# Gate and up projections as seven products of a 2x2 block product in a float32 encoder layer on one core

## The chip, the cores and the metric

The kernel runs on one core of one Trainium2 chip. The metric is the time of one execution on the device in microseconds (us). Three runs of the kernel before gave 1198.27, 1194.62 and 1189.96 us, a median of 1194.62 us. Inside the core five engines work side by side, each on its own queue in order: PE (TensorE, the products), DVE (VectorE), ACT (ScalarE), POOL (GpSimd) and SP, which here only issues transfers.

## The reference

One inference step of an encoder layer: a prompt of 512 tokens and 8 streams of 16 tokens, 640 tokens in all, width 1024. Two attention branches are merged by gates and projected; then comes the feed-forward part that the change is about:

```python
x = x + gate1 * ((gates[:, :, 0] * y_a + gates[:, :, 1] * y_b) @ w_out)
h = modulate(rmsnorm(x, g_norm_ffn), shift2, scale2)
return x + gate2 * ((jax.nn.silu(h @ w_gate) * (h @ w_up)) @ w_down)
```

`w_gate` and `w_up` are 1024 x 2816, `w_down` is 2816 x 1024. All is float32. The hidden width 2816 is 22 blocks of 128.

## The kernel before

Each float32 operand is split in two parts of PE's format: ACT rounds it to the high part (line 86), DVE or POOL subtracts that from the raw value, which gives the low part (line 87). A float32 product is then three matmuls: high by high, low by high, high by low (lines 93 to 95, `mm3`).

The feed-forward part runs over the 22 blocks of the hidden width. For a block `ff_weights` loads 512 KB of `w_gate` and 512 KB of `w_up` (8 slices of 128 x 128 each) into a ring of three raw buffers and splits each 128 x 1024 tile at once. `ff_block` takes 320 of the 640 tokens (tokens 0 to 319, then 320 to 639): 8 slices of the gate product into one PSUM bank, 8 of the up product into another, three matmuls each, then silu on ACT (line 1245), the product on DVE (line 1248) and the split into `aT`, `aTl`. That is 96 matmuls of 128 x 320 a block. After blocks 8, 16 and 22 the down projection adds its 512-column products to the residual `x1` (lines 1279 and 1280).

Ahead of it stands the output projection: for each of five tiles of 128 tokens 24 matmuls, then the new residual, its statistics (`h2_stats`: sum of squares, `rsqrt`, the scaled copy `xn`), and 8 transposes with the modulation and the split (`h2_cols`). `h2_cols(t - 1)` is called after `h2_stats(t)`. The first two blocks' first token half needs tiles 0 to 2 only. And ahead of that stands the merge of the two branches (`w_o_a`, `w_o_b`), whose first weights go into the raw ring `wstA`, which lives through the whole kernel.

The queues are laid out by a list scheduler from the program's text, its priorities and an estimate of each instruction; each engine then runs its list in order and waits on semaphores. So a row that waits holds back all rows behind it on its engine.

Of the kernel before, what the change touches and what calls it, by code (L numbers as in the profile page):

```python
# [8 lines left out]
F32 = mybir.dt.float32  # L9
# [39 lines left out]
def layer_kernel(  # L49
# [42 lines left out]
    def mm3(out, lh, ll, rh, rl, start, stop):  # L92
        T.matmul(out, lh, rh, start=start, stop=False)  # L93
        T.matmul(out, lh, rl, start=False, stop=False)  # L94
        T.matmul(out, ll, rh, start=False, stop=stop)  # L95
# [70 lines left out]
    wa = ctx.enter_context(pool("wstA", side="right"))  # L166

    def load_raw(src, shape, rows=P, given=P):
        n = shape[0] * shape[1]
        raw = wa.tile([P, 1024], F32, tag="w_raw", bufs=3, name=nm("wraw"))[:rows, :n]  # L170
        rv = raw.rearrange("p (k n) -> p k n", k=shape[0])
        if given < rows:
            G.memset(raw, 0.0)
        nc.sync.dma_start(rv[:given], src)
        return raw, rv

    def load_kv_up(c0):
        raw = wa.tile([P, 1024], F32, tag="w_raw", bufs=3, name=nm("wraw"))
# [897 lines left out]
    wb_cm = pool("wstB2", side="right")  # L1076
    wb = wb_cm.__enter__()
    AB = (wa, wb)
    gp_cm = pool("gatebc", side="right")
    gp = gp_cm.__enter__()  # L1080
# [6 lines left out]
    def ada_rows(c0):  # L1087
        raw = wa.tile([P, 1024], F32, tag="w_raw", bufs=3, name=nm("wraw"))
# [4 lines left out]
    def gate_rows(c0, scale):  # L1093

        raw = ada_rows(c0)
        hi = wa.tile([P, 1024], F32R, tag="w_hi", bufs=3, name=nm("whi"))[0:AR, :]
        lo = wa.tile([P, 1024], F32R, tag="w_lo", bufs=3, name=nm("wlo"))[0:AR, :]
        split(hi, lo, raw)
        out = []
        for v in range(2):  # L1100
            g_ = gp.tile([P, DM], F32, tag=f"gate{v}", name=nm("gate"))
            for c in range(2):
                cc = slice(c * 512, (c + 1) * 512)
                ps = mm_tile()
                T.matmul(ps, selr[:, v * P:(v + 1) * P], hi[:, cc], start=True, stop=False)  # L1105
                T.matmul(ps, selr[:, v * P:(v + 1) * P], lo[:, cc], start=False, stop=True)  # L1106
# [4 lines left out]
    with pool("mwork") as mw:  # L1111
# [10 lines left out]
        for bg in range(4):  # L1122
            wo = [granule(AB[br], wo_v[br][:, :, bg * 256:(bg + 1) * 256], [4, 256]) for br in range(2)]
            for bl in range(2):
# [35 lines left out]
    h2T = h2p.tile([P, KD, NT], F32R, tag="h2T", name="h2T")  # L1160
    h2Tl = h2p.tile([P, KD, NT], F32R, tag="h2Tl", name="h2Tl")
# [4 lines left out]
    sq = ow.tile([P, 2, TT], F32, tag="sq", name="sq")  # L1166
    xns = {}

    def h2_stats(t):
# [4 lines left out]
        xn = ow.tile([P, DM], F32, tag="xn", bufs=2, name=nm("xn"))  # L1174
# [3 lines left out]
    def h2_cols(t):  # L1178
        tsl = slice(t * P, (t + 1) * P)
        for b in range(2):  # L1180
# [19 lines left out]
            split(h2T[:, kb_, tsl], h2Tl[:, kb_, tsl], hf_.rearrange("p (k n) -> p k n", k=4))  # L1200
# [4 lines left out]
    def ff_weights(fb, eng=None):  # L1205
        cs_ = slice(fb * P, (fb + 1) * P)
        return granule(wa, wg_v[:, :, cs_], [KD, P], eng=eng) + granule(wb, wu_v[:, :, cs_], [KD, P], eng=eng)

    ffw = []
    for c in range(2):  # L1210
        cc = slice(c * 512, (c + 1) * 512)
        ws = []
        for g in range(4):
            hi, lo = granule(AB[g % 2], w_out_v[:, 2 * g:2 * g + 2, cc], [2, 512])
            ws += [(hi[:, j, :], lo[:, j, :]) for j in range(2)]
        for t in range(TT):
# [121 lines left out]
```

## Time and profile before

| | before |
|---|---|
| median of three runs | 1194.62 us (1189.96 to 1198.27) |
| the profiled execution's own time | 1189.51 us |
| its span, first to last instruction | 1187.7 us |
| mean granted clock of TensorE | 0.992 of 2.4 GHz |
| matmuls in the feed-forward part | 2112 of 128 x 320 (gate, up), 660 of 128 x 512 (down) |

The busy time of an engine is the time in which at least one of its instructions ran. A matmul's own duration overlaps with its neighbours, so the pace of PE is read from counts per stretch, not from the mean of one. "Idle before, releaser" behind a row is the time the engine stood still ahead of it and what ended it.

### The profile page before, as it was taken

To read this page: it belongs to the slowest core of one execution; us is meant where nothing else is said; L and a number is where in the kernel's file an instruction comes from. 1 tells how busy PE (TensorE), PEld (TensorE's weight loads), DVE (VectorE), ACT (ScalarE), POOL (GpSimd) and SP (SyncE) were. 2 spreads that over 40 slices of the span, in tenths; PEclk is the share of its full clock that TensorE was granted. 3 is DMA by queue.
4 is the path that set the end of the run, shared out by engine and by line. 5 is a ranking of instruction groups with operands and counts; after the bars stand their busy time and mean duration, and the time that the engine had idled before them with its cause. 6 is when DMAs were issued, how large, how long until landed. Compare 5 with 4: busy or idle time off the path is not lost. (4 is left out here: it accounts for less than half of the span.)

```text
span 1187.7 us, 19117 instructions
## 1 busy us (share of the span) xinstructions
PE 1141.2 (96%) x7427; PEld 1032.0 (87%) x7427; DVE 594.5 (50%) x1436; ACT 477.6 (40%) x1014; POOL 78.8 (7%) x178
## 2 busy tenths in 40 slices
PE   7899999999999999999798998999999999999998
PEld 6668988999887788888698888999889999889996
DVE  3688565847775663555455256323343323433233
ACT  4575543446664553566633265322122222112210
POOL 0010001010000000111022221000000000000000
PEclk9999999999999999999999999999999999999999
DMA  8832344587656446575685122422124222222211
GB/s 268 297 99 76 113 147 135 168 237 198 183 163 198 116 146 202 192 238 195 191 273 190 36 69 71 125 71 72 36 74 118 76 82 79 71 71 72 72 44 62
DMA packets 156388, 158.13 MB, mean 133 GB/s; under 512 B 24794, under 2 KB 115463, under 8 KB 156298
## 3 DMA queue, kind: packets, MB, share of 16 engines
q1 hardware_dynamic: 156298, 156.92, 42.6%
q8 instruction: 58, 0.95, 0.3%
q14 instruction: 32, 0.26, 0.1%
HBM read 136.59 MB, written 20.30 MB: 132 GB/s over the span
## 5 line engine op out<-in xcount | busy, mean ns | idle before, releaser
L86 ACT CAST whi<-wraw 128x1024 fp32r<-128x1024 f32 (+3 forms) x120 | 123.2, 1032 | 253.8 <-PE mm L95 110.4
L93 PE MATMUL mm<-h2T,whi 128*128 128x320 f32 x704 | 217.6, 310 | 0.0
L94 PE MATMUL mm<-h2Tl,whi 128*128 128x320 f32 x704 | 217.5, 309 | 0.0
L95 PE MATMUL mm<-h2T,wlo 128*128 128x320 f32 x704 | 217.5, 309 | 0.0
L87 DVE TENSOR_TENSOR wlo<-wraw,whi 128x1024 fp32r<-128x1024 f32 (+3 forms) x116 | 138.9, 1198 | 127.0 <-ACT whi L86 125.0
L93 PEld LDWEIGHTS mm<-h2T,whi 128*128 128x128 f32 x704 | 132.5, 189 | 0.2
L94 PEld LDWEIGHTS mm<-h2Tl,whi 128*128 128x128 f32 x704 | 132.3, 188 | 0.1
L95 PEld LDWEIGHTS mm<-h2T,wlo 128*128 128x128 f32 x704 | 132.2, 188 | 0.0
L93 PE MATMUL mm<-whi,aT 128*128 128x512 f32 x220 | 85.5, 389 | 0.0
L95 PE MATMUL mm<-whi,aTl 128*128 128x512 f32 x220 | 85.4, 389 | 0.0
L94 PE MATMUL mm<-wlo,aT 128*128 128x512 f32 x220 | 85.4, 389 | 0.0
L93 PE MATMUL mm<-hT_hi,whi 128*128 128x320 f32 x256 | 83.7, 327 | 1.0 <-ACT whi L86 1.0
L1248 DVE TENSOR_TENSOR sg<-mm,sg 128x320 f32<-128x320 f32 x44 | 21.6, 492 | 121.0 <-PE mm L95 119.0
L95 PE MATMUL mm<-hT_hi,wlo 128*128 128x320 f32 x256 | 81.0, 317 | 0.0
L93 PE MATMUL mm<-whi,hT_hi 128*128 128x512 f32 (+3 forms) x240 | 79.6, 333 | 0.9 <-ACT jk L333 0.9
L94 PE MATMUL mm<-hT_lo,whi 128*128 128x320 f32 x256 | 80.3, 314 | 0.0
L95 PE MATMUL mm<-whi,hT_lo 128*128 128x512 f32 (+3 forms) x240 | 79.4, 332 | 0.0
L94 PE MATMUL mm<-wlo,hT_hi 128*128 128x512 f32 (+3 forms) x240 | 79.3, 331 | 0.0
L1279 DVE TENSOR_TENSOR tmp<-mm,gate 128x512 f32<-128x512 f32 x30 | 20.7, 690 | 79.9 <-PE mm L95 79.9
L93 PEld LDWEIGHTS mm<-hT_hi,whi 128*128 128x128 f32 x256 | 49.2, 192 | 4.9 <-issue 2.1
L86 ACT CAST aT<-sg 128x320 fp32r<-128x320 f32 x44 | 20.1, 457 | 78.7 <-DVE sg L1248 78.7
L95 PEld LDWEIGHTS mm<-hT_hi,wlo 128*128 128x128 f32 x256 | 49.3, 193 | 0.6 <-DVE mx L775 0.4
(328 smaller groups left out, 2345.7 us busy)
## 6 DMA issues: line engine op xcount, KB each, us to landing
adaw<-in_w_ada_dram SPq DMA_DIRECT2D x48, 512.0 KB
wraw<-in_w_in_dram SPq DMA_DIRECT2D x28, 512.0 KB
wraw<-in_w_gate_dram SPq DMA_DIRECT2D x22, 512.0 KB
wraw<-in_w_up_dram SPq DMA_DIRECT2D x22, 512.0 KB
wraw<-in_w_down_dram SPq DMA_DIRECT2D x22, 512.0 KB
lat<-in_cache_kv_latent_dram SPq DMA_DIRECT2D x16, 512.0 KB
wraw<-in_cache_band_v_dram SPq DMA_DIRECT2D x16, 512.0 KB
kn<-in_cache_band_k_dram SPq DMA_DIRECT2D x16, 512.0 KB
```

The costliest lines, as they stand in the source:

```text
L86: S.copy(hi, src)
L87: (eng or V).tensor_tensor(out=lo, in0=src, in1=f(hi), op=ALU.subtract)
L93: T.matmul(out, lh, rh, start=start, stop=False)
L94: T.matmul(out, lh, rl, start=False, stop=False)
L95: T.matmul(out, ll, rh, start=False, stop=stop)
L1248: V.tensor_tensor(out=sg, in0=pu[:, :HALF], in1=sg, op=ALU.mult)
L1279: V.tensor_tensor(out=tmp, in0=ps, in1=gate2[t // 4][:, cc], op=ALU.mult)
```

## The change

The products of a block become a 2x2 block product: the rows are the gate block and the up block, the columns two halves of the tokens, the inner dimension two halves of 512. Seven products of 128 x 512 by 512 x 320 give what eight did, with sums and differences of weight quarters (`s1`, `a11`, `s4`, `a21`, made by POOL and DVE for each block) and of activation quarters (`hB`, `hS`, made once). A token half is now 64 tokens of each of the five tiles, so every product reads all tiles. A block's seventh product is issued within the next block (`last_product`). Block 0 keeps eight products. The down projection runs after 5, 10, 14, 18 and 22 blocks, from a ring of six tiles of hidden activations, in pairs of banks. All operands come from one pool `wops` of 512-column tiles, opened after the attention in the place of `wstA`; it has four raw buffers. `h2_cols(t)` follows `h2_stats(t)` directly.

```diff
-    wa = ctx.enter_context(pool("wstA", side="right"))
+    wa_cm = pool("wstA", side="right")
+    wa = wa_cm.__enter__()
...
     sb_cm.__exit__(None, None, None)
-    wb_cm = pool("wstB2", side="right")
-    wb = wb_cm.__enter__()
+    wa_cm.__exit__(None, None, None)
+
+    wa = ctx.enter_context(pool("wops", side="right"))
+    raws[0] = 4
+
+    def operand(src, n=512):
+        hi = wa.tile([P, 512], F32R, tag="op_hi", bufs=12, name=nm("ophi"))[:, :n]
+        lo = wa.tile([P, 512], F32R, tag="op_lo", bufs=11, name=nm("oplo"))[:, :n]
+        split(hi, lo, src)
+        return hi, lo
...
+    hB = [h2p.tile([P, 3, 4, HALF], F32R, tag=f"hB{i}", name=f"hB{i}") for i in range(2)]
...
+            quarter.append(hf_.rearrange("p (k a x) -> p a k x", k=4, a=2))
+        (b11, b12), (b21, b22) = [(h[:, 0], h[:, 1]) for h in quarter]
+        split(hB[0][:, 0, :, q], hB[1][:, 0, :, q], b11)
+        split(hB[0][:, 1, :, q], hB[1][:, 1, :, q], b21)
+        split(hB[0][:, 2, :, q], hB[1][:, 2, :, q], b22)
+        t1, t2, t3, k12 = [hT_[:, i, :, q] for i in range(4)]
+        G.tensor_copy(k12, b12)
+        for o, a, b in ((t1, b12, b11), (t2, b22, t1), (t3, b22, b12)):
+            G.tensor_tensor(out=o, in0=a, in1=b, op=ALU.subtract)
...
                 h2_stats(t)
-                if t > 0:
-                    h2_cols(t - 1)
-                if t in (1, 3):
-                    ffw.append(ff_weights(len(ffw), G))
-    h2_cols(4)
+                h2_cols(t)
...
+    hS = [tsum.tile([P, 4, 4, HALF], F32R, tag=f"hS{i}", name=f"hS{i}") for i in range(2)]
+    for i in (3, 1, 0, 2):
+        split(hS[0][:, i], hS[1][:, i], hT_[:, i])
...
+        def product(bank, w, h, i, start=True, stop=True, more=None):
+            for k in range(4):
+                ks = slice(k * P, (k + 1) * P)
+                mm3(bank[:, :HALF], w[0][:, ks], w[1][:, ks], h[0][:, i, k, :], h[1][:, i, k, :],
+                    start and k == 0, stop and k == 3, not start if more is None else more)
...
+            for k in range(0, 4, 2):
+                k2 = slice(k, k + 2)
...
+                V.tensor_tensor(out=t4, in0=f(hB[0][:, 1, k2]), in1=f(hS[0][:, 1, k2]), op=ALU.subtract)
+                V.tensor_tensor(out=t4, in0=t4, in1=f(hB[1][:, 1, k2]), op=ALU.add)
+                V.tensor_tensor(out=t4, in0=t4, in1=f(hS[1][:, 1, k2]), op=ALU.subtract)
+                split(hS[0][:, 3, k2], hS[1][:, 3, k2], t4)
+
+        def last_product():
+
+            if tail:
+                pa, u1, a22, o = tail.pop()
+                product(pa, operand(a22), hS, 3, start=False)
+                V.tensor_tensor(out=u1, in0=pa[:, :HALF], in1=u1, op=ALU.mult)
+                split(o[0], o[1], u1.rearrange("p (t x) -> p t x", x=64))
+
+        def ff_block(fb):
+
+            new_hidden()
+            a11, a12, a21, a22 = quarters(fb)
+            sums = fw.tile([P, 2, 512], F32, tag="sums", name=nm("sums"))
+            s1, s4 = sums[:, 0], sums[:, 1]
+            G.tensor_tensor(out=s1, in0=a21, in1=a22, op=ALU.add)
+            V.tensor_tensor(out=a21, in0=a11, in1=a21, op=ALU.subtract)
+            o11 = operand(a11)
+            G.tensor_tensor(out=a11, in0=s1, in1=a11, op=ALU.subtract)
+            G.tensor_tensor(out=s4, in0=a12, in1=a11, op=ALU.subtract)
+            pa, pb, pc = mm_tile(), tr_tile(), tr_tile()
+            product(pa, o11, hB, 0)
+            u1 = part(pa, "u1", 2)
+            product(pb, operand(s1), hS, 0)
+            u5 = part(pb, "u5")
+            last_product()
+            product(pa, operand(a11), hS, 1, start=False)
+            u2 = part(pa, "u2")
+            product(pb, operand(s4), hB, 2, start=False)
+            V.tensor_tensor(out=u2, in0=pb[:, :HALF], in1=u2, op=ALU.add)
+            S.activation(out=u2, in_=u2, func=AF.Silu)
+            product(pc, operand(a12), hB, 1)
+            V.tensor_tensor(out=u1, in0=pc[:, :HALF], in1=u1, op=ALU.add)
+            S.activation(out=u1, in_=u1, func=AF.Silu)
+            product(pa, operand(a21), hS, 2, start=False)
+            u3 = part(pa, "u3")
+            G.tensor_tensor(out=u3, in0=u3, in1=u5, op=ALU.add)
+            G.tensor_tensor(out=u2, in0=u2, in1=u3, op=ALU.mult)
+            hidden(1, u2)
...
+        first_block()
+        ends = [0, 5, 10, 14, 18]
+        for fb in range(1, NFF):
+            ff_block(fb)
+            if fb == 1:
+                gate2 = gate_rows(5 * DM, 1.0)
+            if fb in ends:
+                i = ends.index(fb)
+                down(ends[i - 1], fb)
+        last_product()
+        down(ends[-1], NFF)
```

`part` copies a bank's 320 columns out with ACT while the bank goes on collecting; `u1`, `u2` and `u3` are three states of one bank.

Where rows move, first place: SP's queue at the end of the attention. `wraw_1724` holds the last weights that the attention reads, `g` are the gates of the merge. Before:

```order
L218 DMA ada_d_92<-adar_1714_7404 105x512
L180 DMA wraw_1724_7460<-in_w_kv_up_dram 128x8x64
L174 DMA wraw_1729_7548<-in_w_o_a_dram 128x4x256
L174 DMA wraw_1732_7554<-in_w_o_b_dram 128x4x256
L1129 DMA g_1735_7560<-gate_d_93 128x640
```

Now:

```order
L222 DMA ada_d_92<-adar_1714_7404 105x512
L184 DMA wraw_1724_7460<-in_w_kv_up_dram 128x8x64
L1147 DMA g_1739_7569<-gate_d_93 128x640
L1147 DMA g_1740_7571<-gate_d_93 128x640
L1147 DMA g_1749_7639<-gate_d_93 128x640
L1147 DMA g_1750_7641<-gate_d_93 128x640
L178 DMA wraw_1729_7549<-in_w_o_a_dram 128x4x256
L178 DMA wraw_1734_7559<-in_w_o_b_dram 128x4x256
```

The first two loads of the merge stand behind the gates now, and the first of them waits for the last matmul that reads `wraw_1724`, since the new pool takes that memory; before, each waited for a matmul of an earlier step.

Second place: PE's queue at the end of the output projection (`mT` operands); `xn` is a tile's scaled residual. Before, from the last tile's last matmuls on:

```order
L94 MATMUL mm_1932_8688<-wlo_1879_8421,mT_7503 128x512
L95 MATMUL mm_1932_8688<-whi_1878_8420,mTl_7504 128x512
L139 MATMUL tr_1939_8730<-ident_65,xn_1921_8650 128x128 x4
L139 MATMUL tr_1941_8742<-ident_65,xn_1921_8650 128x128 x4
L93 MATMUL mm_1949_8780<-h2T_8225,whi_1899_8534 128x320
...
L139 MATMUL tr_1943_8754<-ident_65,xn_1938_8728 128x128 x4
L139 MATMUL tr_1945_8764<-ident_65,xn_1938_8728 128x128 x4
```

Now:

```order
L95 MATMUL mm_1958_8782<-oplo_1913_8491,mT_7504 128x512
L96 MATMUL mm_1958_8782<-ophi_1912_8490,mTl_7505 128x512
L140 MATMUL tr_1954_8752<-ident_65,xn_1953_8750 128x128 x4
L140 MATMUL tr_1956_8762<-ident_65,xn_1953_8750 128x128 x4
L140 MATMUL tr_1965_8824<-ident_65,xn_1964_8822 128x128 x4
L140 MATMUL tr_1967_8832<-ident_65,xn_1964_8822 128x128 x4
L94 MATMUL mm_1981_8890<-hB0_8262,ophi_1973_8874 128x320
```

The fifth tile's transposes stood 66 rows behind the fourth's, among the products of the first blocks; now they stand ahead of the first product.

Third place: ACT's queue in the change where block 1 begins, and DVE's beside it. `mm_1996` is block 1's bank, `t4` the pieces of the last activation sum, `ophi_2000` the operand of block 1's second product (`s1`).

```order
L86 CAST aT_1969_8868<-u_1986_8995 128x5x64
L1278 COPY u1_1999_9042<-mm_1996_9027 128x320
L86 CAST hS0_8854<-t4_1988_9006 128x640
L86 CAST ophi_2000_9044<-sums_1993_9018 128x512
L86 CAST ophi_2003_9062<-wraw_1991_9014 128x512
L86 CAST ophi_2006_9080<-sums_1993_9018 128x512
```

```order
L1315 TENSOR_TENSOR t4_1988_9006<-t4_1988_9006,hS1_8855 128x640
L87 TENSOR_TENSOR hS1_8855<-t4_1988_9006,hS0_8854 128x640
L1333 TENSOR_TENSOR wraw_1992_9016<-wraw_1991_9014,wraw_1992_9016 128x512
L87 TENSOR_TENSOR oplo_2001_9045<-sums_1993_9018,ophi_2000_9044 128x512
L87 TENSOR_TENSOR oplo_2004_9063<-wraw_1991_9014,ophi_2003_9062 128x512
```

Before, all of a block's weights were split in rows that stood ahead of the block's first silu; here the operand of the second product stands behind a copy of the first product's bank, and on DVE behind the last activation sum.

## Rows read from the trace of the kernel before

**Rows 1.** The page: busy time by engine, then the chain that ended last, by engine.

```profile
PE 1141.2 (96%) x7427; PEld 1032.0 (87%) x7427; DVE 594.5 (50%) x1436; ACT 477.6 (40%) x1014; POOL 78.8 (7%) x178
...
PE 45%; DVE 1%; ACT 0%; issue 0%
```

**Rows 2.** Windows, gate and up alone: us; busy (count) by engine; clock, DMA, GB/s.

```profile
920.00:960.00 40.00, 40.00 (x275) 40.00 (x274) 12.47 (x17) 9.97 (x17) 0.00 (x0) 1.00 0.25 73
960.00:1000.00 40.00, 40.00 (x275) 40.00 (x274) 11.76 (x17) 9.81 (x17) 0.00 (x0) 1.00 0.25 80
```

**Rows 3.** Groups by line and shape, 640 to 1188 us: busy, mean ns | idle before.

```profile
L93 PE MATMUL mm<-h2T,whi 128*128 128x320 f32 x704 | 217.6, 310 | 0.0
...
L1248 DVE TENSOR_TENSOR sg<-mm,sg 128x320 f32<-128x320 f32 x44 | 21.6, 492 | 121.0 <-PE mm L95 119.0 <-ACT sg L1245 2.0
...
L1280 DVE TENSOR_TENSOR x<-x,tmp 128x512 f32<-128x512 f32 x30 | 20.8, 692 | 1.0
...
L86 ACT CAST aT<-sg 128x320 fp32r<-128x320 f32 x44 | 20.1, 457 | 78.7 <-DVE sg L1248 78.7
L1245 ACT ACTIVATE sg<-mm 128x320 f32<-128x320 f32 x44 | 19.1, 434 | 43.1 <-PE mm L95 43.1
...
L1223 POOL TENSOR_TENSOR x<-x,tmp 128x512 f32<-128x512 f32 x5 | 6.5, 1295 | 15.8 <-DVE tmp L1222 15.8
...
L86 ACT CAST h2T<-hfull 128x512 fp32r<-128x512 f32 x10 | 5.7, 617 | 0.0
```

**Rows 4.** In order of time, PE, end of the attention, then SP and ACT.

```profile
583.45 3.62 PE L1066 MATMUL mm<-olatT,wraw 128*128 128x128 f32 x30 [0.62 <-DMA wraw<-in_w_kv_up_dram]
588.73 0.42 PE L93 MATMUL mm<-oh,whi 128*128 128x320 f32 x1 [1.66 <-ACT whi L86]
...
577.86 2.47 SPq L174 DMA_DIRECT2D wraw<-in_w_o_a_dram  x1
...
589.96 0.40 SPq L174 DMA_DIRECT2D wraw<-in_w_o_a_dram  x1
...
593.49 1.06 ACT L86 CAST whi<-wraw 128x1024 fp32r<-128x1024 f32 x1 [0.63 <-DMA wraw<-in_w_o_a_dram]
```

**Rows 5.** In order of time, PE, from the output projection to the first block.

```profile
718.63 1.97 PE L139 MATMUL tr<-ident,xn 128*128 128x128 f32 x8 [3.29 <-ACT xn L1175]
720.25 1.39 PE L93 MATMUL mm<-h2T,whi 128*128 128x320 f32 x4
...
730.28 1.03 PE L139 MATMUL tr<-ident,xn 128*128 128x128 f32 x8
```

**Rows 6.** Windows around it.

```profile
719.00:720.00 1.00, 1.00 (x7) 1.00 (x6) 0.96 (x2) 1.00 (x4) 0.00 (x0) 0.50 0.41 94
...
722.00:724.00 2.00, 2.00 (x16) 2.00 (x15) 0.78 (x3) 1.73 (x4) 0.00 (x0) 1.00 0.65 156
```

**Rows 7.** In order of time, DVE and ACT: a tile's residual, its scaled copy, modulation.

```profile
696.34 0.69 DVE L1222 TENSOR_TENSOR tmp<-mm,gate 128x512 f32<-128x512 f32 x1 [0.59 <-PE mm L95]
...
699.92 1.16 ACT L1175 ACTIVATE xn<-x,rs 128x1024 f32<-128x1024 f32 x1 [0.81 <-DVE rs L110]
...
732.27 1.28 DVE L1199 TENSOR_TENSOR hfull<-hfull,B 128x512 f32<-128x512 f32 x2
```

**Rows 8.** In order of time, POOL beside DVE, two places.

```profile
637.80 0.88 POOL L1144 TENSOR_TENSOR t<-t,t 128x320 f32<-128x320 f32 x1 [1.56 <-DVE t L1141]
641.92 1.73 POOL L1144 TENSOR_TENSOR t<-t,t 128x320 f32<-128x320 f32 x1 [3.24 <-DVE t L1141]
...
641.69 1.22 DVE L87 TENSOR_TENSOR wlo<-wraw,whi 128x1024 fp32r<-128x1024 f32 x1
...
711.53 4.73 POOL L87 TENSOR_TENSOR wlo<-wraw,whi 128x1024 fp32r<-128x1024 f32 x2 [20.13 <-ACT whi L86]
...
712.11 1.83 DVE L1172 TENSOR_TENSOR ss<-sq 128x1 f32<-128x1 f32 x1 [0.45 <-ACT tmp L1224]
...
714.30 0.16 DVE L107 RECIPROCAL rs<-rst 128x1 f32<-128x1 f32 x1 [0.17 <-ACT rst L106]
```

More of the change, by code (lines that the diff above doesn't have):

```diff
@@ L90, in split, with mm3 @@
             (eng or V).scalar_tensor_tensor(out=lo, in0=src, scalar=scale, in1=f(hi), op0=ALU.mult, op1=ALU.subtract)
[L92 to L95, printed above, removed]
+    def mm3(out, lh, ll, rh, rl, start, stop, more=False):
+        T.matmul(out, lh, rh, start=start, stop=False, skip_group_check=more)
+        T.matmul(out, lh, rl, start=False, stop=False, skip_group_check=more)
+        T.matmul(out, ll, rh, start=False, stop=stop, skip_group_check=more)
     def rsqrt(out, ss, inv, pl, n):
@@ L177, in load_kv_up @@
     def load_kv_up(c0):
[L178 removed]
+        raw = wa.tile([P, 1024], F32, tag="w_raw", bufs=raws[0], name=nm("wraw"))
         for k in range(2):
@@ L1075, in layer_kernel, with operands @@
     sb_cm.__exit__(None, None, None)
-    wb_cm = pool("wstB2", side="right")
-    wb = wb_cm.__enter__()
-    AB = (wa, wb)
-    gp_cm = pool("gatebc", side="right")
-    gp = gp_cm.__enter__()
+    wa_cm.__exit__(None, None, None)
[6 more added lines that the diff above has]
+        return hi, lo
+    def operands(src, shape):
+        raw = load_raw(src, shape)[0]
+        return [operand(raw[:, i * 512:(i + 1) * 512]) for i in range(shape[0] * shape[1] // 512)]
+    gp = ctx.enter_context(pool("gatebc", side="right"))
     mT_cm = pool("mT", side="right")
@@ L1095, in gate_rows @@
         raw = ada_rows(c0)
-        hi = wa.tile([P, 1024], F32R, tag="w_hi", bufs=3, name=nm("whi"))[0:AR, :]
-        lo = wa.tile([P, 1024], F32R, tag="w_lo", bufs=3, name=nm("wlo"))[0:AR, :]
-        split(hi, lo, raw)
+        parts = []
+        for c in range(2):
+            hi = wa.tile([P, 512], F32R, tag="op_hi", bufs=12, name=nm("ophi"))[0:AR, :]
+            lo = wa.tile([P, 512], F32R, tag="op_lo", bufs=11, name=nm("oplo"))[0:AR, :]
+            split(hi, lo, raw[:, c * 512:(c + 1) * 512])
+            parts.append((hi, lo))
         out = []
@@ L1122, in layer_kernel @@
         for bg in range(4):
-            wo = [granule(AB[br], wo_v[br][:, :, bg * 256:(bg + 1) * 256], [4, 256]) for br in range(2)]
+            wo = [operands(wo_v[br][:, :, bg * 256:(bg + 1) * 256], [4, 256]) for br in range(2)]
             for bl in range(2):
@@ L1213, in layer_kernel @@
         for g in range(4):
-            hi, lo = granule(AB[g % 2], w_out_v[:, 2 * g:2 * g + 2, cc], [2, 512])
-            ws += [(hi[:, j, :], lo[:, j, :]) for j in range(2)]
+            ws += operands(w_out_v[:, 2 * g:2 * g + 2, cc], [2, 512])
         for t in range(TT):
```

119 lines of the change are left out of this document (61 added, 58 removed).

## The prediction, made before the changed kernel ran

> **What bounds the kernel now.** I read the page first: PE is busy 1141.2 us of 1187.7, DVE 594.5, ACT 477.6, POOL 78.8, and of the chain that ended last PE is the only engine with a share worth naming [rows 1]. A share is an average over stages, so I then cut windows out of the feed-forward part, where only gate and up products run. There PE is busy 40.00 of 40 us at a granted clock of 1.00, DVE 12.47, ACT 9.97, POOL 0 [rows 2]. PE works through 275 matmuls in 40 us, so one 128 x 320 matmul costs 40 / 275 = 0.1455 us. (Its own duration, 310 ns [rows 3], overlaps with its neighbours and is not its price.) Each product removed is worth its full 0.1455 us, as long as the three other engines, which all get more to do, stay ahead of PE. PE's waits ahead of this part are small and known: 1.66 us before the merge [rows 4] and 3.29 us before the last transposes of the output projection [rows 5]. The change touches both places.
>
> The sum is made against the profiled execution's own 1189.51 us; the median of the runs, 1194.62, stands 5.1 above it.
>
> **A, the products.** Before: 22 blocks x 96 = 2112 (704 on each of three lines [rows 3]). After: block 0 keeps 96, the other 21 have 7 products x 12 = 84, together 1860. 252 fewer x 0.1455 = **-36.7 us**. The order has those 252 rows fewer, so that the change does not do what it says is excluded. The 660 matmuls of the down projection stay. They now go in five groups in place of three, so 50 sums leave PSUM where 30 did, 20 x 2 x 0.692 us on DVE [rows 3], covered as the old ones are: the next matmuls use other banks. Bytes loaded stay the same, at a quarter of the DMA engines' time [rows 2]: nothing.
>
> **B, attention to merge.** Before, the first merge weights had been issued at 577.86 and PE began the merge 1.66 us after its last attention matmul [rows 4]. Now they take memory that this matmul reads, so the load starts when it ends, at 583.45 + 3.62 = 587.07. A load of that size stands in the same rows from issue to cast: 593.49 - 589.96 = 3.5 us. With a cast of 512 columns, 0.62 [rows 3], the merge starts near 591.2 in place of 588.73: +2.5, and PE stands some 4.1 us. After the idle 3.29 us the clock was 0.50, and it was 1.00 again three to four us later [rows 5, 6]; half speed over some 3 us of work is 1.5 more. B = +4, between +1 (the gates' loads ahead in SP's queue cost nothing, a fourth raw buffer returns some) and +6 (behind them the load lands late).
>
> **C, output projection to block 0.** Each product now reads all five tiles, so the last tile's chain lies bare. Before, the first product started at 720.25, after transposes that began 718.63 - 3.29 = 715.34 was PE's last work [rows 5]: 4.9 us, and the fifth tile's transposes took 1.03 later. Now: last product to residual 0.25 (bounded by the 0.59 that DVE had waited [rows 7]); residual to the end of `xn` 699.92 + 1.16 - 696.34 = 4.75 [rows 7]; transposes 1.97 at the low clock [rows 5]; two halves of modulation at 0.64 an operation, two operations each, 2.5 [rows 7]; the split of the first quarter 0.6. That is 10.0, so 10.0 - 4.9 - 1.0 = +4.1, and half-speed products behind the longer gap add a little. C = +4.5. POOL now also runs four operations a tile in this chain, and where it ran beside DVE a 128 x 1 sum of two inputs took 1.83 us, a one-input operation 0.16 [rows 8]. So the upper end is +9; the lower is +2, where the first quarter's work overlaps the transposes.
>
> **D, the start of block 1.** ACT's queue has a copy of the first product's bank, then the cast of the last activation sum (640 columns, twice 0.43), then the cast of the second product's operand; DVE has a 640-column subtraction and two of 512 ahead of the low part. From rows 3: 0.43 + 0.86 + 0.62 on ACT and 0.98 + 2 x 0.69 on DVE behind it, some 3.8 us with PE standing. The third operand's difference on POOL (1.3) waits for DVE in turn. D = +5, from +2 (the second product's operand early) to +8 (both waits in full).
>
> **E, 20 blocks like it.** A block costs PE 84 x 0.1455 = 12.2 us. From rows 3, DVE: 8 operations of 512 at 0.69, 5 of 320 at 0.49, 8.0. ACT: 7 casts at 0.62, 4 copies and silus at 0.43, 2 + 2 casts and activations at 0.46, 7.9 at most. POOL: 3 sums at 1.295, and 2 of 320 at 0.88 [rows 8], 5.6. Each alone is below 12.2. But DVE and POOL do not run free of each other: POOL's sum took 0.88 alone and 1.73 while a DVE subtraction of two SBUF inputs ran, and that 1.83 against 0.16 says the same for DVE [rows 8]. DVE's operations with both inputs in SBUF are 8 x 0.69 + 2 x 0.49 = 6.5; with POOL's 5.6 they need 12.1 of 12.2 us, one after the other. The down groups give slack: they use neither POOL nor much DVE, and with twelve high operands and four raw buffers the next block's work can go ahead into them. I take 0.25 us a block, E = +5; 0 is the lower end, the second rival the upper.
>
> The Trainium skill ("SBUF — State Buffer", section "Who interferes with whom") has a rule that speaks against this change: a DVE instruction with two SBUF inputs and a GpSimd instruction that reads SBUF shut each other out for the whole instruction, and one with a single SBUF input does not. Rows 8 agree, with 1.73 against 0.88 and 1.83 beside 0.16. By the rule E would be near 0 if every hold is absorbed, for 12.1 is still under 12.2, and up to +28 if none is.
>
> Copies, the second gate's rows and the last down group: nothing, since PE has other products there and DVE the same two operations after the last.
>
> **Sum:** -36.7 + 4 + 4.5 + 5 + 5 = -18.2. From 1189.5 that is 1171.3, from the median 1176.4; I take 1174 between them.
>
> **The rivals.**
>
> Forecast, 0.55: PE keeps the pace but for the boundaries; 1162 to 1184 with the bounds of B to D.
>
> Second, 0.20: DVE and POOL together set the pace, because their work is serial and strictly ordered in each queue. If all of it is, a block takes 8.0 + 5.6 = 13.6 us, 1.4 more than PE's 12.2, x 20 = 28 in place of E's 5: -36.7 + 13.5 + 28 = +4.8, 1194 to 1199: no change. For it: the holds in rows 8. Against it: 13.6 counts the PSUM readers too, and the slack of the down groups.
>
> Third, 0.13, slower: ACT's order. The cast of `s4`, which comes from POOL, stands in ACT's queue ahead of the copy that must empty a bank before PE may add the next product to it. If POOL's sums come late, the copy does, PE stands, and with it everything that would be freed. The chain from one release to the next is DVE 0.49 + ACT 0.46 + DVE 0.49 + 0.69 + POOL 2 x 1.3 + ACT 0.62 + 0.43 = 5.8 us, against 65 matmuls that stand between them in the order, 9.5 us. It decides once holds add more than 3.7 us to it, that is, with three or four operations held to twice their time. A block of 15 us then gives 20 x 2.8 = 56: -36.7 + 13.5 + 56 = +33, 1222 to 1227. It is slower by over 1% from a block of about 14 us. For it: every product needs an operand of its own, and each engine runs in order. Against: the ring lets operands be made a block ahead.
>
> Fourth, 0.12: the operands are always there, the boundaries half hidden: -36.7 + 1 + 2 + 2 = -31.7, 1158 to 1163.
>
> **Numbers.** Less than 1% (under 12 us: 1182.7 to 1206.6) can't be told from no change by a measurement of this kernel. Faster: 0.53 of the forecast and the fourth, 0.65. Same: the second and the forecast's edge, 0.20. Slower: the third and the second's tail, 0.15. The range from 1157 to 1199 takes in the fourth, the forecast and the second; out are the third and a piece of the second's tail, under 0.2. The forecast's own range is 1162 to 1184.
>
> **What would show it.** In the profile after: 1860 matmuls of 128 x 320; 275 of them in 40 us between boundaries (A, E); about 4 us idle before the first merge matmul and a low clock behind it (B); about 10 us from the last output-projection matmul to the first block's (C); 4 to 6 us idle inside block 1 (D). Fewer than 260 in 40 us, with PE's idle time ended by DVE's low parts or POOL's sums, and DVE's 512-column subtractions well over 692 ns, would be the second rival; idle time ended by ACT's copy of a bank the third. I would be wrong above all if the operands are not made ahead: then E is no longer a small term.

## The result and the profile after

The changed kernel takes 1180.60 us, the median of 7 runs (1179.27 to 1183.97); the kernel before took 1192.23 in the runs beside them (1188.78 to 1198.27). The ratio is 0.9904, 95% interval 0.9876 to 0.9932: about 1% faster. The forecast was 1174 with a range of 1157 to 1199. The profiled execution took 1179.59 us against 1189.51, 9.9 us less where the sum said 18.2.

First the page: busy time by engine, then the chain that ended last, by engine. It answers [rows 1].

```profile
PE 1116.3 (95%) x7175; PEld 1001.2 (85%) x7175; DVE 744.7 (63%) x1686; ACT 563.5 (48%) x1256; POOL 221.3 (19%) x299
...
PE 33%; DVE 0%; ACT 0%; issue 0%
```

PE executes 252 matmuls fewer (7427 to 7175); DVE, ACT and POOL all do more. Then a window between two down groups, in which only seven-product blocks run, the answer to [rows 2]: us; busy (count) of PE, PE's weight loads, DVE, ACT, POOL; clock, DMA, GB/s.

```profile
872.00:912.00 40.00, 40.00 (x275) 40.00 (x274) 28.36 (x43) 23.19 (x49) 15.20 (x13) 1.00 0.31 92
```

DVE has gone from 11.76 to 28.36 us, POOL from 0 to 15.20, and PE still gets through 275 matmuls and stands nowhere. Between the first two down groups 401 matmuls take 59.03 us, which puts their starts 0.1468 us apart. So the steady blocks cost what their matmuls cost, and the loss lies at the seams, where one stage hands over to the next. PE's longer waits from the merge on, in order of time:

```profile
592.24 0.63 PE L94 MATMUL mm<-oh,ophi 128*128 128x320 f32 x1 [5.73 <-ACT ophi L86]
...
716.72 1.25 PE L140 MATMUL tr<-ident,xn 128*128 128x128 f32 x8 [2.18 <-ACT xn L1195]
722.82 1.97 PE L140 MATMUL tr<-ident,xn 128*128 128x128 f32 x8 [4.85 <-ACT xn L1195]
729.50 0.64 PE L94 MATMUL mm<-hB,ophi 128*128 128x320 f32 x1 [4.71 <-ACT hB L86]
752.43 0.64 PE L94 MATMUL tr<-hS,ophi 128*128 128x320 f32 x1 [4.45 <-ACT ophi L86]
784.74 0.41 PE L94 MATMUL mm<-hS,ophi 128*128 128x320 f32 x1 [1.83 <-ACT u L1278]
```

They are the start of the merge, the last two tiles before the feed-forward part (the third and fourth row are both the fifth tile's chain), and blocks 1 and 3; the expectations below call the last one block 4's, but the bank that it waits for is the third seven-product block's. Behind them PE works at half clock for some us, which idle time does not show. Windows of the same kernel:

```profile
730.00:732.00 2.00, 2.00 (x9) 1.81 (x8) 2.00 (x4) 2.00 (x4) 2.00 (x3) 0.50 0.00 0
...
756.00:758.00 2.00, 2.00 (x9) 2.00 (x9) 1.86 (x4) 2.00 (x5) 0.00 (x0) 0.50 0.00 0
787.00:789.00 2.00, 2.00 (x9) 2.00 (x9) 1.86 (x3) 1.69 (x4) 1.92 (x2) 0.50 0.84 249
...
596.00:598.00 2.00, 2.00 (x10) 2.00 (x9) 0.47 (x1) 1.12 (x2) 0.00 (x0) 0.50 1.04 409
598.00:600.00 2.00, 2.00 (x16) 2.00 (x15) 1.31 (x3) 0.01 (x1) 0.00 (x0) 0.99 1.03 377
```

PE is 2.00 of 2.00 us busy there, yet gets through 9 or 10 matmuls, where 2 us at 1.00 hold 13 to 16. Such a window shows in the clock and the count, not in the busy share.

One loss shows in no wait at all. These are consecutive matmuls of a down group, the kernel before and then the changed one (first column: start).

```profile
1012.18 0.39 PE L93 MATMUL mm<-whi,aT 128*128 128x512 f32 x1
1012.40 0.39 PE L94 MATMUL mm<-wlo,aT 128*128 128x512 f32 x1
1012.63 0.39 PE L95 MATMUL mm<-whi,aTl 128*128 128x512 f32 x1
```

```profile
1012.22 0.40 PE L94 MATMUL mm<-ophi,aT 128*128 128x512 f32 x1
1012.46 0.39 PE L95 MATMUL mm<-oplo,aT 128*128 128x512 f32 x1
1012.69 0.40 PE L96 MATMUL mm<-ophi,aTl 128*128 128x512 f32 x1
```

Over longer pieces of the same groups the starts lie 0.2267 us apart before and 0.2333 after. Times 660 that is 4.4 us. The 320-column matmuls keep 0.1467 in both.

**The ledger**, from the last output-projection matmul's end to the last matmul's end: 715.35 to 1183.19 before, 714.54 to 1172.92 after, 9.5 us less.

| part | us |
|---|---|
| 252 products x 0.1467 | -37.0 |
| output projection to first product, 4.9 to 15.0, less the old fifth transposes (1.03) | +9.0 |
| half clock behind it (2.5, before 0.6) | +1.9 |
| waits of blocks 1 and 3 and of the last down group, 4.45 + 1.83 + 0.35 | +6.6 |
| half clock behind the first two | +4.8 |
| pace of the down products | +4.4 |
| sum | -10.3 |

The measured -9.5 is 0.8 short of this sum, and that 0.8 is unassigned. The half-clock terms are (1 - clock) times each window's length, added up. Ahead of the ledger, from the first instruction to 715.35 and 714.54, 0.8 us went; behind it, from the last matmul to the end of the span, 0.3 came.

### The profile page after: what moved, and what is told of

The parts are those of the page before. It is cut to its first block, busy times and chain, and to the rows that moved or that the text cites. A ratio compares the mean times of both kernels' runs of the same rounds, so it can differ in the third digit from the quotient of the medians.

```text
span 1177.8 us, 19436 instructions
## 1 busy us (share of the span) xinstructions
PE 1116.3 (95%) x7175; PEld 1001.2 (85%) x7175; DVE 744.7 (63%) x1686; ACT 563.5 (48%) x1256; POOL 221.3 (19%) x299
## 5 line engine op out<-in xcount | busy, mean ns | idle before, releaser
L86 ACT CAST ophi<-wraw 128x512 fp32r<-128x512 f32 (+1 forms) x189 | 114.7, 620 | 138.6 <-PE mm L96 56.4
L87 DVE TENSOR_TENSOR oplo<-wraw,ophi 128x512 fp32r<-128x512 f32 (+1 forms) x189 | 150.3, 811 | 41.6 <-PE mm L96 17.1
L94 PE MATMUL mm<-ophi,aT 128*128 128x512 f32 x220 | 87.1, 396 | 0.4 <-DVE u L1323 0.3
L95 PE MATMUL mm<-oplo,aT 128*128 128x512 f32 x220 | 86.9, 395 | 0.0
L96 PE MATMUL mm<-ophi,aTl 128*128 128x512 f32 x220 | 86.0, 395 | 0.0
L94 PE MATMUL mm<-hS,ophi 128*128 128x320 f32 x256 | 80.2, 313 | 1.8 <-ACT u L1278 1.8
L95 PE MATMUL mm<-hS,ophi 128*128 128x320 f32 x256 | 80.2, 314 | 0.0
L96 PE MATMUL mm<-hS,oplo 128*128 128x320 f32 x256 | 79.8, 313 | 0.0
L87 DVE TENSOR_TENSOR wlo<-wraw,whi 128x1024 fp32r<-128x1024 f32 (+2 forms) x36 | 41.0, 1141 | 27.8 <-ACT whi L86 27.0
L95 PE MATMUL tr<-hB,ophi 128*128 128x320 f32 x180 | 56.0, 312 | 0.0
L94 PE MATMUL tr<-hB,ophi 128*128 128x320 f32 x180 | 56.0, 311 | 0.0
L96 PE MATMUL tr<-hB,oplo 128*128 128x320 f32 x180 | 55.2, 311 | 0.0
```

What stands on the lines that cost most here:

```text
L86: S.copy(hi, src)
L87: (eng or V).tensor_tensor(out=lo, in0=src, in1=f(hi), op=ALU.subtract)
L94: T.matmul(out, lh, rh, start=start, stop=False, skip_group_check=more)
L95: T.matmul(out, lh, rl, start=False, stop=False, skip_group_check=more)
L96: T.matmul(out, ll, rh, start=False, stop=stop, skip_group_check=more)
```

## The experiments

The profiled executions of these kernels end the attention between 585.8 us (e2) and 595.0 (e1), 9 us apart, in work that no experiment's edit touches. So beside each ratio to the kernel before stands F, the time of the profiled execution from the last output-projection matmul's end to the end of the span. F comes from one execution of each kernel, but where nothing differs it repeats: the 401 matmuls named above take 59.01 to 59.03 us in the eleven executions that have them in this order. The intervals of the ratios reach some 3 to 6 us to either side, so differences of under 5 us between two changed kernels are read from F alone.

| kernel | median us | ratio to before, 95% | F us |
|---|---|---|---|
| before | 1192.23 | 1 | 472.4 |
| changed | 1180.60 | 0.9904 (0.9876 to 0.9932) | 463.3 |
| e1 shift by 32 bytes | 1176.47 | 0.9869 (0.9841 to 0.9897) | 458.8 |
| e2 own buffers for t4 | 1179.06 | 0.9897 (0.9874 to 0.9920) | 459.0 |
| e3 POOL's rows left out, tiles 4, 5 | 1181.77 | 0.9923 (0.9900 to 0.9945) | 460.5 |
| e4 eight products | 1212.47 | 1.0181 (1.0147 to 1.0214) | 490.6 |
| f1 first merge weights | 1181.37 | 0.9915 (0.9880 to 0.9950) | 464.5 |
| f2 POOL's rows one column in 64, tiles 3 to 5 | 1179.48 | 0.9901 (0.9869 to 0.9934) | 463.4 |
| f3 e2, gate rows late | 1176.19 | 0.9866 (0.9829 to 0.9904) | 459.4 |
| f4 e2, old halves | 1176.77 | 0.9884 (0.9843 to 0.9925) | 459.1 |
| g3 e1 and e2 | 1175.27 | 0.9841 (0.9809 to 0.9872) | 456.8 |
| g1 g3, weight sums on DVE | 1166.42 | 0.9773 (0.9739 to 0.9807) | 448.4 |
| g2 g3, first down group early | 1174.32 | 0.9832 (0.9800 to 0.9864) | 457.4 |
| h1 g1, old halves | 1165.37 | 0.9790 (0.9739 to 0.9841) | 448.6 |

### e1: the pace of the down products

The built program gives each tile's address: `aT` and `aTl` begin 32 bytes past a multiple of 64 before, on one after; the moving weights (`whi`, `ophi`) 32 past in both.

```diff
+    pad = ctx.enter_context(pool("padw"))
+    pad.tile([P, 8], F32, tag="pad", name="pad")
     with pool("fwork") as fw:
```

Expected:

> The hidden activations aT, aTl and the rest of their pool stand 32 bytes further on; nothing else differs from the changed kernel. In the kernel before they began 32 bytes past a multiple of 64, like the weights that the down projection moves past them; in the changed kernel they begin on a multiple of 64. Theory (the pace of the down products hangs on that offset): the spacing of 128x512 down products goes from 0.2333 us back to 0.2267, 660 x 0.0066 = 4.4 us, so about 1175 us where the changed kernel has 1179.6. Rival (it is the six separate tiles, their 64-column writing, or DVE and POOL working beside them): spacing stays 0.2333 and the time within 1 us.

A down group of e1:

```profile
834.17 0.39 PE L96 MATMUL mm<-ophi,aTl 128*128 128x512 f32 x1
834.40 0.39 PE L94 MATMUL mm<-ophi,aT 128*128 128x512 f32 x1
834.62 0.39 PE L95 MATMUL mm<-oplo,aT 128*128 128x512 f32 x1
```

The spacing is back at 0.227 and F falls by 4.5, against 4.4 forecast. The offset sets the pace; the separate tiles and the engines beside it do not. The changed kernel has a second witness: its output projection moves the same pool's operands past `mT`, whose tiles begin 32 past a multiple of 64, and there the starts lie 0.227 apart.

```profile
711.67 0.39 PE L95 MATMUL mm<-oplo,mT 128*128 128x512 f32 x1
711.90 0.39 PE L96 MATMUL mm<-ophi,mTl 128*128 128x512 f32 x1
712.12 0.39 PE L94 MATMUL mm<-ophi,mT 128*128 128x512 f32 x1
```

Whether it is the difference between the two operands' offsets that counts or the stationary one's alone was not tested. The 320-column matmuls speak for the second: their stationary operand begins 32 past throughout, the moving one 32 past (`hS`) or on a multiple of 64 (`hB`), and the spacing is 0.147 either way.

### e2: block 1's start

Block 1's start in the changed kernel, in order of time, DVE, POOL and ACT:

```profile
749.41 0.83 DVE L87 TENSOR_TENSOR hS<-t,hS 128x640 fp32r<-128x640 f32 x1 [0.79 <-ACT hS L86]
...
750.47 1.26 POOL L1332 TENSOR_TENSOR sums<-wraw 128x512 f32<-128x512 f32 x1 [17.99 <-DVE hS L87]
...
751.76 0.62 ACT L86 CAST ophi<-sums 128x512 fp32r<-128x512 f32 x1 [2.38 <-POOL sums L1332]
```

POOL had been free for 17.99 us; what ended its wait is DVE's last read of `t4`, because `t4` and `sums` share one buffer (one tag). e2 parts them, which also makes four pieces of `t4` where two stood:

```diff
-            for k in range(0, 4, 2):
-                k2 = slice(k, k + 2)
-                t4 = fw.tile([P, 2 * 512], F32, tag="sums", name=nm("t4"))[:, :2 * HALF]
+            for k in range(4):
+                t4 = fw.tile([P, 512], F32, tag="tmp", bufs=2, name=nm("t4"))[:, :HALF]
```

Expected:

> The pieces of the last activation sum (t4) go into two 512-column buffers that the down projection uses later, in four pieces of 320 columns, and no longer into the one buffer that a block's weight sums need. Theory (block 1 starts late because its first weight sum waits on POOL for the last read of t4 in the shared buffer): PE's 4.45 us ahead of block 1's second product go to under 1, the 1.83 us before block 4's product with them, since the raw buffers come free earlier, and most of the low clock behind both (4 to 5 us): 8 to 11 us in all, about 1169 to 1172 us. Rival (ACT's and DVE's in-order queues hold the second product's operand whatever the buffer): over 3 us of the gap stay and the time is within 2 us of the changed kernel's. Second rival (loads, not operands, set the ramp): the first gap goes, the second stays or moves: 3 to 6 us.

PE's waits between 740 and 800 us in e2:

```profile
755.85 0.42 PE L94 MATMUL tr<-hB,ophi 128*128 128x320 f32 x1 [1.04 <-ACT u L1278]
765.66 0.41 PE L94 MATMUL mm<-hS,ophi 128*128 128x320 f32 x1 [0.62 <-ACT u L1278]
769.82 0.41 PE L94 MATMUL tr<-hB,ophi 128*128 128x320 f32 x1 [0.38 <-ACT u L1278]
775.89 0.41 PE L94 MATMUL mm<-hS,ophi 128*128 128x320 f32 x1 [1.55 <-ACT u L1278]
788.59 0.41 PE L94 MATMUL mm<-hS,ophi 128*128 128x320 f32 x1 [1.66 <-ACT u L1278]
```

The 4.45 us are gone, so the shared buffer was their cause. But 5.25 us came back in five pieces, all ended by ACT's copy of a bank: the wait that the prediction's third rival named. What is won (4.3 of F; the medians, 1179.06 against 1180.60, are too close to tell apart) is mostly half clock: behind these waits it is 1.00 throughout from 740 to 800 us. In size this is the second rival of the expectation. Its reason, the loads, is one link of a longer chain, as block 3's wait in the changed kernel shows (the load's issue, POOL, then ACT twice):

```profile
777.05 0.37 SPq L178 DMA_DIRECT2D wraw<-in_w_up_dram  x1
...
781.18 1.29 POOL L1332 TENSOR_TENSOR sums<-wraw 128x512 f32<-128x512 f32 x1 [4.70 <-DMA wraw<-in_w_up_dram]
...
782.51 0.62 ACT L86 CAST ophi<-sums 128x512 fp32r<-128x512 f32 x1 [3.49 <-POOL sums L1332]
...
784.28 0.40 ACT L1278 COPY u<-mm 128x320 f32<-128x320 f32 x1
```

The load was issued when one of DVE's low parts had freed a raw buffer (the semaphore came at 777.04). So a late low part makes a late load, a late sum, a late cast and a late copy, and at 784.74 PE goes on.

### e3 and f2: POOL in the last tiles' chain

e3:

```diff
-        G.tensor_copy(k12, b12)
+        if t < 3:
+          G.tensor_copy(k12, b12)
...
```

> POOL's four operations on the activation quarters are left out for the fourth and fifth tile of 128 tokens (their places hold zeros), so that POOL is idle in the last tiles' chain. Theory (POOL holds DVE's operations with two SBUF inputs there): the three low parts of the fourth tile, 2.68 us now, take 3 x 0.42, the fifth tile's rs chain some 1 us less, and the first product starts 3 to 4 us earlier than 13.0 us after the last output-projection work; 3 to 4 us less in all. Rival (the chain's length is its own, with contention beside the path): under 1 us.

e3 told nothing about POOL's part in that chain: without the last tiles' rows the splits of `hS` no longer depended on them and moved ahead of the fifth tile's work. ACT and PE in e3:

```profile
722.55 2.42 ACT L86 CAST hS<-hsum 128x1280 fp32r<-128x1280 f32 x2
...
734.02 0.64 PE L94 MATMUL mm<-hB,ophi 128*128 128x320 f32 x1 [5.98 <-ACT hB L86]
```

The first product came 16.8 us behind the last output-projection matmul, not 15.0. (F is 2.8 lower all the same: `hS` was ready early, and block 1's wait of 4.45 us is not there.) f2 keeps the rows in their places and leaves out all but one column in 64:

```diff
+        if t > 1:
+            t1, t2, t3, k12, b11, b12, b22 = [v[:, :, 0:1] for v in (t1, t2, t3, k12, b11, b12, b22)]
         G.tensor_copy(k12, b12)
```

> POOL's four operations a tile on the activation quarters work on one column in 64 for the third, fourth and fifth tile (the other columns hold zeros), so the rows stand where they stood but POOL is hardly busy. Theory (POOL holds DVE in the last tiles' chain): from the end of the last output-projection matmul to the first product 11 to 12 us in place of 15.0, the fourth tile's three low parts 1.2 us in place of 2.68, the two-input operations of the fifth tile's rs chain 0.16 in place of 0.68. Rival (the rows of the fourth tile that stand ahead of the fifth's on DVE make the chain long, whatever POOL does): 14 us or more.

DVE's rows for the fifth tile's scale and the fourth tile's low parts, the changed kernel:

```profile
719.92 0.68 DVE L110 SCALAR_TENSOR_TENSOR rst<-rst,rsv 128x1 f32<-128x1 f32 x1
...
724.53 2.68 DVE L87 TENSOR_TENSOR hB<-hfull,hB 128x256 fp32r<-128x256 f32 x3 [0.61 <-ACT hB L86]
```

f2, DVE and then PE:

```profile
721.84 0.15 DVE L110 SCALAR_TENSOR_TENSOR rst<-rst,rsv 128x1 f32<-128x1 f32 x1
...
728.72 0.63 PE L94 MATMUL mm<-hB,ophi 128*128 128x320 f32 x1 [2.47 <-ACT hB L86]
...
751.79 0.64 PE L94 MATMUL tr<-hS,ophi 128*128 128x320 f32 x1 [4.75 <-ACT ophi L86]
...
779.71 0.42 PE L94 MATMUL mm<-hS,ophi 128*128 128x320 f32 x1 [1.01 <-ACT u L1281]
...
794.24 0.42 PE L94 MATMUL mm<-hS,ophi 128*128 128x320 f32 x1 [1.85 <-ACT u L1281]
```

728.72 - 716.65 = 12.1 us where it was 15.0: POOL's holds made 2.9 us of that chain. And F is 463.4 against 463.3. What was won at 729 us had gone again by 800, in longer waits of blocks 1 to 3: 8.8 us in all where the changed kernel has 6.3.

### e4: the seven products themselves

```diff
         for fb in range(1, NFF):
-            ff_block(fb)
+            first_block(fb)
```

> All 22 blocks take the eight products of the first block; pools, rings, token halves and down groups stay as changed, and the weight sums, t4 and the postponed product are gone. Theory (a product removed is worth its full 0.1467 us and the steady blocks lose nothing to DVE and POOL): 252 matmuls more, +37.0, less the waits of block 1 and block 4 with their low clock, some 11: about 1205 us, and no product of the 320 kind further apart than 0.1467. Rival (the two-engine work of the seven products costs something in each block, 0.25 us or more): the difference to the changed kernel is 5 us or more below that, 1200 or less.

From its first product to the end of the span e4 takes 1206.0 - 733.88 = 472.1 us, the changed kernel 1177.8 - 729.50 = 448.3. The difference is 23.8. The removed products give 37.0, less 11.4 for the changed kernel's waits and the half clock behind them: 25.6. Some 2 us are unexplained. They do not lie in the steady blocks: e4's 480 matmuls between its first two down groups take 70.62 us, 0.1468 apart, the same as the changed kernel's 401. So the rival, 0.25 us a block, is out. e4 also lost 3.5 us more than the changed kernel in the gap ahead of that, which the forecast of 1205 did not have.

### f1: the merge's first weights

```diff
+                if bg == 0:
+                    raw = mw.tile([P, 1024], F32, tag=f"wfirst{br}", name=nm("wfirst"))
+                    nc.sync.dma_start(raw.rearrange("p (k n) -> p k n", k=4), src)
```

> The merge's first two weight loads go into two buffers of the merge's own pool, which takes memory that the attention gives back earlier, and stand ahead of the gates in SP's queue; all else as in the changed kernel. Theory (PE stands 5.7 to 7.7 us ahead of the merge because those loads cannot start before the last attention matmul, and then works at half clock for some 6 us): the idle time falls to under 2 us, the clock stays at 1.00, and from the last attention matmul to the last output-projection matmul it takes 121 to 123 us where the changed kernel has 128.0: 5 to 7 us less in all. Rival (the loads still land late, or the cast is held by other work on ACT): over 4 us of idle time stay, under 2 us in all.

PE in f1:

```profile
592.55 0.64 PE L94 MATMUL mm<-oh,ophi 128*128 128x320 f32 x1 [2.87 <-ACT ophi L86]
605.55 0.41 PE L94 MATMUL mm<-oh,ophi 128*128 128x320 f32 x1 [2.38 <-DVE t L1167]
```

Half of the wait moved back 13 us. From the last attention matmul to the last output-projection matmul it took 127.7 us, in the changed kernel 128.0, in the kernel before 128.3. The twelve executions whose merge is the changed kernel's spread from 126.6 to 129.6, so none of these differences says anything, but the 121 to 123 of the theory is out. The rival held.

### f3, f4, g3, g2, g1, h1: what sets the first blocks' pace

f3 moves one condition (`if fb == 1` before the second gate's rows becomes `if fb == 4`) on top of e2:

> As the kernel with its own buffers for t4, and the second gate's rows (one raw buffer, two casts, two low parts, four copies) come after block 4 in place of block 1. Theory (their raw buffer pushes the loads of blocks 2 to 4 one place back in the ring): PE's waits behind ACT's bank copies in blocks 1 to 4, 5.25 us in that kernel, fall under 2 us, about 4 us less in all. Rival (the ramp is a chain of load, POOL's sum, DVE's difference, cast in each block, with all of the queues in order): the waits stay at 4 us or more, the time within 2 us of that kernel's.

Six waits of 4.97 us in all stayed; F 459.4 against 459.0. The rival's forecast held; its chain is the one shown under e2. f4 gives a token half 320 tokens in a row again, on top of e2:

```diff
-        q = slice(t * 64, (t + 1) * 64)
...
+        for half, c0, n, q0 in ((0, 0, 128, t * 128),) if t < 2 else (
+                ((0, 0, 64, 256), (1, 64, 64, 0)) if t == 2 else ((1, 0, 128, t * 128 - 320),)):
```

> As the kernel with its own buffers for t4, and a token half is again 320 tokens in a row, so that block 0's first half needs the first three tiles only. Theory (the last tiles' chain lies bare because each product reads all tiles): from the end of the last output-projection matmul to the first product 5 to 7 us in place of 15.0, no half clock behind it, 9 to 11 us less than that kernel, about 1169. Rival (the sums hS and t4 end no earlier, so PE only waits later, in block 0's second half or ahead of block 1's second product): 6 us or more of the gain come back as idle time there, 0 to 4 us less in all.

The first product came 4.2 us behind the last output-projection matmul, and then:

```profile
738.65 0.63 PE L94 MATMUL mm<-hS,ophi 128*128 128x320 f32 x1 [5.87 <-ACT hS L86]
```

Block 0's second half waited for `hS`, further waits followed, F 459.1: the rival. Starting block 0 earlier does not make the sums `hS` end earlier, and they are what PE then waits for. g3 puts e1 and e2 together:

> The shift of 32 bytes and the own buffers for t4 together. Theory (one changes the pace of the down products, the other PE's waits in blocks 1 to 4, and they add): from the end of the last output-projection matmul to the end of the span 463.3 us in the changed kernel goes to 463.3 - 4.4 - 4.3 = 454.6, the time to about 1171 us. Rival (products that move on faster meet the same late operands): the shift's 4.4 us come back as waits, 458 to 459 us. The down groups all lie behind the waits, so this is unlikely.

F is 456.8, some 2 us under either and 2.2 short of their sum. The shift's spacing of 0.227 is there, but a wait of 1.75 us at 794.23 brought 1.7 us of half clock, which e2's trace does not have. g2 moves the first down group from behind block 5 to behind block 3, on top of g3 (`ends = [0, 3, 8, 13, 18]`):

> As the kernel with shift and own buffers for t4, and the down projection runs after 3, 8, 13, 18 and 22 blocks. Theory (the waits of blocks 1 to 4 are a backlog of operands that the first down group, which needs none of POOL, works off): two of the four blocks move behind the first down group and wait no more, the waits fall from 5.3 to 3 us or less, 2 to 3 us less in all. Rival (the down group's own ten operands on DVE and ACT, now earlier, make the backlog longer): no gain, or waits within the first down group.

g3's four waits in blocks 1 to 3 (5.24 us) became three (3.23), and new ones came, at the first down group and, small, at 850 us:

```profile
798.45 0.51 PE L94 MATMUL mm<-ophi,aT 128*128 128x512 f32 x1 [2.27 <-DVE tmp L1374]
```

No gain. g1 moves the three weight sums of a block from POOL to DVE, on top of g3:

```diff
-            G.tensor_tensor(out=s1, in0=a21, in1=a22, op=ALU.add)
+            V.tensor_tensor(out=s1, in0=a21, in1=a22, op=ALU.add)
...
-            G.tensor_tensor(out=a11, in0=s1, in1=a11, op=ALU.subtract)
-            G.tensor_tensor(out=s4, in0=a12, in1=a11, op=ALU.subtract)
+            V.tensor_tensor(out=a11, in0=s1, in1=a11, op=ALU.subtract)
+            V.tensor_tensor(out=s4, in0=a12, in1=a11, op=ALU.subtract)
```

> As the kernel with shift and own buffers for t4, and DVE makes the three weight sums of a block in place of POOL. Theory (in blocks 1 to 4 the chain of load, POOL's sum, DVE's difference, two more sums on POOL, and their holds on DVE's low parts make operands late): PE's waits between 750 and 800 us, 5.3 us in the kernel with t4's own buffers, fall under 2.5, 2 to 4 us less from the last output-projection matmul on. Rival (DVE's own work there, 10 of 12 us, is the bound, and this adds 2.1 us a block to it): the waits grow to 6 us or more.

Blocks 1 to 4, first g3's window and its low parts on DVE (count | busy, mean ns), then g1's:

```profile
750.00:800.00 50.00, 44.67 (x282) 42.87 (x282) 43.27 (x62) 29.46 (x64) 23.70 (x17) 0.97 0.28 85
...
L87 DVE TENSOR_TENSOR oplo<-wraw,ophi 128x512 fp32r<-128x512 f32 x21 | 20.1, 977 | 0.1
```

```profile
750.00:800.00 50.00, 50.00 (x339) 49.66 (x338) 46.75 (x81) 34.82 (x72) 6.86 (x6) 1.00 0.34 100
...
L87 DVE TENSOR_TENSOR oplo<-wraw,ophi 128x512 fp32r<-128x512 f32 x25 | 18.8, 767 | 0.9 <-ACT ophi L86 0.6 <-PE mm L96 0.2
```

PE works 50.00 of 50 us, through 339 matmuls in place of 282, and all its waits in blocks 1 to 3 are gone. DVE gets 81 operations done in 46.75 us where 62 took 43.27: relieved of POOL, a low part takes 767 ns, not 977. F falls by 8.4. The theory had said 2 to 4, and not counted that the half clock goes with the waits: 5.2 of waits and 1.7 of half clock make 6.9; 1.5 is unassigned. From g1's first product on, 1168.6 - 735.15 = 433.5 us; its matmuls at their own spacing are 1860 x 0.1467 + 660 x 0.2267 + 1.8 (the eight matmuls that spread the second gate) = 424.3; half clock at the start (2.5), a wait ahead of the last down group (0.6) and the end after the last matmul (4.6) make 432.0. About 1.5 us is left.

h1 is g1 with f4's halves:

> The kernel with shift, own buffers for t4 and the weight sums on DVE, and besides a token half of 320 tokens in a row, so that block 0's first half needs the first three tiles only. Theory (with POOL's sums gone from blocks 1 to 4 operands are ahead, so the earlier start is kept): from the last output-projection matmul to the first product 5 to 7 us in place of 15.0, at most 6 us of waits ahead of block 0's second half, and 448.4 us from there to the end of the span goes to 442 to 445, about 1162. Rival (DVE, 10.9 to 12 of 12 us busy in that stretch already, is the bound): the waits come back in blocks 0 to 2, 447 us or more.

```profile
734.54 0.64 PE L94 MATMUL mm<-hS,ophi 128*128 128x320 f32 x1 [5.86 <-ACT hS L86]
```

F 448.6: the rival again. Its median and g1's can't be told apart, so g1, the simpler, is the version to keep. It beats the kernel before by 2.3% (1.9 to 2.6).

## Why the prediction held, and where its sum was off

The time fell inside the range and the direction was forecast, by the mechanism named: a product removed is worth its spacing (A: -36.7 forecast, -37.0 by the ledger, and e4 bears it out to 2 us; the 0.1455 behind the forecast divides by a count that takes in matmuls cut by the window's ends, the starts lie 0.1467 apart). The gain was about half of the forecast one, because four terms were mis-sized and one was missing.

| term | forecast | measured |
|---|---|---|
| A, the products | -36.7 | -37.0 |
| B, the merge | +4 | 0, to within some 1.5 |
| C, output projection to block 0, with half clock | +4.5 | +10.9 |
| D, block 1, wait and half clock | +5 | +7.5 |
| E, the other blocks: block 3's wait and half clock, the last group's wait | +5 | +3.9 |
| pace of the down products | 0 | +4.4 |

B and E were put 5 us too high, C, D and the pace 13.3 too low. That the errors partly cancel is luck, and so is how near the total came; C lies above its own upper end of +9. The prediction doubted that under 1% could be told from no change; the 11.6 us could, with an interval of 0.7 to 1.2%.

**B, the merge (+4).** Its own wait was 5.73 us against a forecast 4.1, and 2.9 us of half clock followed; but the stretch to the end of the output projection became no longer: 128.0 against 128.3, in a spread of 3 us (f1). I charged the new wait and credited nothing. The kernel before lost 1.66 us ahead of the merge and 0.70 + 0.81 + 0.95 + 2.20 within it, with 1.7 of half clock behind the last, 8.0 in all; the changed kernel has 5.73 and 2.9, 8.6, and the waits within the merge are gone. f1 shows the same trade: take a wait away in front and one appears behind. What paces the merge's first blocks (from 592 to 620 us the DMA share is 0.96 in the changed kernel and 1.01 in f1) was not isolated.

**C, output projection to block 0 (+4.5).** 15.0 us where the working had 10.0. The duration sum took each row at its undisturbed length. f2 shows that POOL's holds make 2.9 of the missing 5. The rest fits the fourth tile's rows, which stand among the fifth's on DVE and ACT: the fifth tile's residual started 1.45 us behind PE, not 0.25, and from it to the end of `xn` even f2 takes 6.1 us where the working had 4.75. No run tested that part. With 1.9 of half clock C was 10.9.

**D, block 1 (+5).** The wait was of the forecast size, 4.45, by luck: its cause was none of those named, not the queue orders of ACT and DVE, but one buffer that `t4` and the weight sums share (e2). The working had followed the rows and not the tags. (The terms that it lists add up to 4.3, not 3.8.) Half clock behind it, 3.0, was not counted.

**E, the other blocks (+5).** In the steady blocks it is 0. DVE is busy 28.36 and POOL 15.20 of 40 us, low parts take 845 ns in place of the 692 of the same shape [rows 3], and PE does not wait. The changed kernel's group from 875 to 910 us:

```profile
L87 DVE TENSOR_TENSOR oplo<-wraw,ophi 128x512 fp32r<-128x512 f32 x17 | 14.0, 845 | 3.5 <-PE tr L96 1.8 <-PE mm L96 1.7
```

But in blocks 1 to 3, which start with no operands in store, the second and third rivals were right, as one thing: POOL's sums and their holds make operands late (g1), and with them the loads that wait for a raw buffer, and the lateness reaches PE through ACT's queue, as the copy of a bank behind a cast that waits (e2). That fits C's shortening in f2 and f4 buying nothing. The Trainium skill ("SBUF — State Buffer", section "Who interferes with whom") has DVE instructions with two SBUF inputs contend with GpSimd instructions that read SBUF; that one shuts the other out for its whole length, as the prediction puts it, the page says of DVE's two-port modes. The runs agree in kind, and no run here measures the length of a hold: 0.68 us in the changed kernel against 0.15 in f2 for the same row, 977 ns in g3 against 767 in g1 for a low part. g1 does not tell POOL's holds from the longer chain through two engines.

**Missing:** 4.4 us by the offset of 32 bytes that `aT` and `aTl` lost (e1). The 660 down products were set at no cost because their number and shape stayed.

## What to carry to other kernels

When work is taken off the bound engine, price the seams before the steady state: a wait of some two us or more cost once as idle time and, nearly always here, again as half clock, and where operands start from nothing, a gap that was closed in one place opened in the next until the making of operands was sped up. Follow buffers (tags) as well as queues when a start is priced, for a shared one is an order of its own. And when tiles move, compare the spacing of rows that were not changed.

## What the runs showed of the hardware

- A float32 matmul of 512 columns by a 128 x 128 stationary operand was spaced 0.2267 us with the stationary operand 32 bytes past a multiple of 64 and 0.2333 with it on one, the moving operand 32 past in both. The 320-column matmuls, stationary operand 32 past, were spaced 0.147 with the moving operand 32 past and on a multiple alike.
- From 560 us on, where PE had been at full clock, the granted clock stayed at 1.00 behind waits of up to 1.69 us. From 1.70 to 1.97 us it went either way: it fell to 0.50, that is 1.2 GHz, behind 1.70 (g3, 583.17), 1.75 (g3, 794.23), 1.83 (the changed kernel, 784.74) and 1.85 (f2), and did not behind 1.72 (g3, 781.45), 1.84 (the changed kernel, 578.00) and 1.97 (f3). Behind all of 2.18 us and more it fell, for 3 to 6 us of work. So five waits of 1 us can be cheaper than one of two.
- The same 512-column sum took 1.3 to 1.6 us on POOL and 0.69 to 0.86 on DVE. In g1's window from 750 to 800 us DVE made sums for 10.1 us, and its busy time was only 3.5 us longer than g3's.
